# Modulation loads issued by GpSimd, and three groups of layer 0's output projection moved from whole to three-pass products

## The chip, the cores and the metric

The kernel runs on one core of a Trainium2 chip. A core has a matrix engine (TensorE, PE), a vector engine (VectorE, DVE), a scalar engine (ScalarE, ACT), GpSimd (POOL) and SyncE (SP), each with a list of instructions of its own that it works through in order. Sixteen DMA engines carry the transfers that an engine's list starts. The metric is the device time of one execution in microseconds (us), as the median of several runs.

## The reference

A decoder trunk of two layers, width 2048, 256 tokens, all in float32. Cut to what matters:

```python
c_act = silu(c)
for l in range(2):
    mod = c_act @ w_mod[l] + b_mod[l]                  # 2048 x 12288 per layer
    shift1, scale1, gate1, shift2, scale2, gate2 = split(mod, 6)
    h = rms_norm(x, norm1_gain[l]) * (1 + scale1) + shift1
    x = x + gate1 * mixer(h, w_in[l], ..., w_out[l])   # one input and one output projection
    h = rms_norm(x, norm2_gain[l]) * (1 + scale2) + shift2
    x = x + gate2 * (silu(h @ w_gate[l]) * (h @ w_up[l])) @ w_down[l]   # inner width 5632
return rms_norm(x, final_norm_gain)
```

The mixer cuts the projected columns into three sorts of heads: gated linear attention (GLA, 512 output columns), sliding-window softmax attention with sinks (1024 columns) and gated DeltaNet (512 columns). Their outputs stand side by side, 2048 wide, and go through `w_out`.

## The kernel before, in words

The 256 tokens are two blocks of 128 rows. All weights are read from HBM once, in tiles of 128 rows by up to 1024 columns (512 KB).

The order of the work is that of the Python code, as a scheduler turns it into one list for each engine: it takes the code's order as priority and fills each engine's list by its own estimate of when things are ready. Each list is then fixed, and an instruction in it waits by semaphores for data and for free buffers. A DMA stands in the list of the engine that issues it, and whatever is behind it in that list waits with it.

*Weights.* `stream()` walks jobs (a pair of 512-column segments, an index k of 128 rows), and `load()` inside it issues each weight tile on SP (L323). There are two forms of product:

- three-pass: the tile `raw` is rounded to `wh` by ScalarE (L330), VectorE forms the rest `wl` = `raw` - `wh` (L331), and PE adds three products in a fast rounded format (`wh` with both halves of the activations, `wl` with one). `raw` has 3 buffers, `wh` and `wl` 3 each.
- whole: the tile is multiplied as it is, in plain float32, each product as two PE instructions in the trace; nothing is rounded or split. The tiles then take turns in the buffers of `raw`, `wh` and `wl`, nine in all.

For the output projection the constant `WHOLE_OUT` names, by layer, the groups of four k whose products are whole: group 0 is GLA (k 0 to 3), 1 and 2 are softmax attention (k 4 to 11), 3 is DeltaNet (k 12 to 15). The projection has 16 k and two halves of 1024 columns, so 32 jobs, k 4 to 15 first. Activations of a three-pass group are split in the same way, by `split_mix`, between softmax attention and GLA.

*Modulation.* `mod_segment` computes `c_act @ w_mod` for one stretch of columns. For each 128 rows it loads a tile of `w_mod` (L220), and VectorE multiplies it by a column of `c_act` and adds it to an accumulator (L223). The accumulator is cleared by GpSimd (L212), and its first row is filled with `b_mod` by a 4 KB load (L213). When all 16 steps are done, PE sums over the partitions (L238 for gates, L248 for the others), into `fin`; VectorE turns that into columns `mod` (L250 to L256).

Layer 0's first shift and scale are "early": 512 columns wide, 256 KB loads, tiles named `g`, 128 loads in all. The other 20 segments have 1024 columns and 16 loads of 512 KB each, named `mraw` (2 buffers) and `acc` (2 buffers). They are spread over the other work: `tick()` is called as the streams go on and releases a step at a rate that depends on the stage (`RATE_A`, `RATE_OUT`, `RATE_FFN` and the like). `hold` ties one load after each second norm to the norm's end, by a tiny GpSimd copy into its buffer (L218). Before the change SP issues all of these loads, between the weights.

*GpSimd* also computes the inverse square roots of all norms (L408), the negated sinks (L891) and some clears.

Of the kernel before, what the change touches and what calls it, by code (L numbers as in the profile page):

```python
# [19 lines left out]
P = 128  # L20
# [22 lines left out]
WHOLE_IN = (True, False)  # L43
WHOLE_A = (3, 0)
RATE_LAST = 1.6
WHOLE_OUT = ((0, 1, 2, 3), ())
XN_ACT = ((False, False), (False, False))

FIN_LAG = 4
# [54 lines left out]
def trunk(ctx: ExitStack, tc, x, cT, pos, small, consts, b_mod, w_mod, w_in, w_gk, w_out,  # L104
# [22 lines left out]
    def tl(pool, shape, tag, dt=F32, bufs=None):  # L127
        return pool.tile(shape, dt, tag=tag, name=nm(tag), bufs=bufs)
# [11 lines left out]
    V, A, G, TE, SY = nc.vector, nc.scalar, nc.gpsimd, nc.tensor, nc.sync  # L140
# [41 lines left out]
    for name, turn in (("sin", 0.0), ("cos", 0.25)):  # L182
        n = tl(kp, [P, NB, 8], "turns" + name)
# [17 lines left out]
    def mod_segment(l, part, k0, nk):  # L201

        width = nk * P
        early = l == 0 and part in (SHIFT1, SCALE1)
        rows = (512 if early else 1024) // width
        st = {}

        def step(i):
            c0 = part * D + k0 * P
            if i == 0:  # L210
                st["acc"] = scr[1]() if early else tl(accp, [P, 1024], "acc")
                G.memset(st["acc"][:, :width], 0.0)  # L212
                SY.dma_start(st["acc"][0:1, :width], b_mod[l:l + 1, c0:c0 + width])  # L213
            acc = st["acc"][:, :width]
            n = min(rows, KD - i)
            raw = scr[1]() if early else tl(modp, [P, 1024], "mraw")
            if hold:
                G.tensor_copy(raw[:, 0:1], hold.pop())  # L218
            raw = raw[:, :n * width].rearrange("p (a n) -> p a n", a=n)
            SY.dma_start(raw, w_mod[l, i * P:(i + n) * P, c0:c0 + width]  # L220
                         .rearrange("(a p) n -> p a n", p=P))
            for a in range(n):
                V.scalar_tensor_tensor(acc, raw[:, a], c_act[:, i + a:i + a + 1], acc,  # L223
                                       ALU.mult, ALU.add)
            if i + n == KD:
                fins.append([FIN_LAG, lambda: finish(acc)])

        def finish(acc):
            if part in (GATE1, GATE2):
                g = tl(gatep, [P, 1024], "gate")  # L230
                for j in range(width // 512):
                    src = acc[:, j * 512:(j + 1) * 512]
                    t = tl(modp, [P, 2, 512], "mraw", F32R)
                    A.activation(t[:, 0], src, AF.Copy)
                    V.tensor_tensor(t[:, 1], src, t[:, 0].bitcast(F32), ALU.subtract)
                    ps = tl(psf, [P, 512], "fin")
                    for i in range(2):
                        TE.matmul(ps, ones_r, t[:, i], start=i == 0, stop=i == 1)  # L238
                    A.activation(g[:, j * 512:(j + 1) * 512], ps, AF.Copy)
                    gate_row[l, part, k0 // 4 + j] = g[:, j * 512:(j + 1) * 512]  # L240
                return
            t = tl(smp, [P, nk], f"mod{part}_{k0}_{nk}")
            sums = tl(smp, [P, nk], f"sums{nk}")
            for j in range(0, nk, 4):
                ps = tl(psf, [P, 512], "fin")
                n = min(4, nk - j)
                for i in range(n):
                    TE.transpose(ps[:, i * P:(i + 1) * P],  # L248
                                 acc[:, (j + i) * P:(j + i + 1) * P], ident)
                V.tensor_reduce(sums[:, j:j + n],  # L250
                                ps[:, :n * P].rearrange("p (a b) -> p a b", a=n), AX.X, ALU.add)
            if part in (SHIFT1, SHIFT2):
                V.tensor_copy(t, sums)
            else:
                o = (0 if part == SCALE1 else KD) + k0
                V.scalar_tensor_tensor(t, sums, 1.0, gains[:, l, o:o + nk],  # L256
                                       ALU.add, ALU.mult)
            for j in range(nk):
                mod_col[l, part, k0 + j] = t[:, j:j + 1]

        return [((l, part), lambda i=i: step(i)) for i in range(0, KD, rows)]


# [113 lines left out]
    def ahead(wsp_n, hm_n):  # L377
        return (None,) * wsp_n + (at_hm,) * hm_n
# [7 lines left out]
    def split(src, scale=None):  # L386

        h = tl(hmp, [P, 4, P], "hm", F32R)
        lo = tl(hmp, [P, 4, P], "hm", F32R)
        h2, lo2 = (t.rearrange("p a b -> p (a b)") for t in (h, lo))  # L390
        if scale is None:
            A.activation(h2, src, AF.Copy)
            V.tensor_tensor(lo2, src, h2.bitcast(F32), ALU.subtract)
        else:
            A.activation(h2, src, AF.Copy, scale=scale)
            V.scalar_tensor_tensor(lo2, src, scale, h2.bitcast(F32), ALU.mult, ALU.subtract)
        return h, lo
# [91 lines left out]
    def to_mix(l, key, ps, gain=None):  # L489
        if key[1] == 0 and 0 not in WHOLE_OUT[l]:  # L490
            mix[key] = split(ps, gain)
            return
        t = mix[key] if key in mix else tl(hmp, [P, 4, P], "hm")
        A.activation(t.rearrange("p a b -> p (a b)"), ps, AF.Copy,
                     scale=1.0 if gain is None else gain)
        mix[key] = t
# [23 lines left out]
    def split_mix(l, group):  # L520
        if group not in WHOLE_OUT[l]:
            for blk in range(NB):
                mix[blk, group] = split(mix[blk, group].rearrange("p a b -> p (a b)"))
# [425 lines left out]
    def layer(l):  # L949
# [158 lines left out]
        for ks in (range(4, 16), range(0, 4)):  # L1108
            final = ks[0] == 0
            if final:  # L1110
# [3 lines left out]
                           blk, j, ps, half, final)) for half in range(2)]  # L1114
            stream(groups, ks, lhs_mix, whole=[k for k in ks if k // 4 in WHOLE_OUT[l]],
                   tail=() if not final else TAIL_WHOLE if 0 in WHOLE_OUT[l] else
                   ahead(*TAIL_OUT))
# [100 lines left out]
```

## Time and profile before

| | us |
|---|---|
| median of 3 runs (2582.32 to 2587.12) | 2582.44 |
| the profiled execution | 2585.34 |
| its span | 2583.5 |
| PE busy | 2432.7 |
| VectorE busy | 1714.4 |
| ScalarE busy | 1053.5 |
| GpSimd busy | 58.2 |

The mean granted PE clock was 0.986 of full. Windows give, for a stretch of the span, each engine's busy time with its instructions in brackets (PE, its weight loads PEld, DVE, ACT, POOL), then the granted clock, the mean busy share of the 16 DMA engines and GB/s. A row of a group of instructions gives line, engine, operation, result <- operands, shapes and count; busy time and mean ns; idle time of the engine just ahead of them and what ended it. A row of waits gives total us, times and the longest. A timeline row gives start, duration, engine, line, operation, and in brackets the idle time ahead of it and what ended that. SPq is the list of DMAs on SP.

The stages by the span's time: early modulation and input projection of layer 0 to 390 us, GLA and output projection to 560, second norm to 592, FFN of layer 0 to 1360; input projection of layer 1 from 1390 to 1510, its attention, GLA and output projection to 1830, its FFN to 2560.

### The profile page before, as it was taken

What the parts mean: (1) busy time and instruction counts of PE and PEld (TensorE: products, weight loads), DVE (VectorE), ACT (ScalarE), POOL (GpSimd) and SP (SyncE); (2) the same over time, 40 slices, a digit from 0 to 9 for tenths busy, and PEclk for the clock granted to TensorE, in tenths of its full rate; (3) what the DMA queues carried; (4) which work ended last, traced back from release to release, by engine and by line L of the source; (5) the groups of instructions that cost most, each with busy time, mean ns of one, the idle gap of its engine ahead of it and who ended that gap; (6) DMA issues with size and microseconds to landing.
All of it is one profiled execution on the core that took longest, in us unless ns stands there. A gap on an engine that the chain in (4) does not pass through costs nothing.

```text
span 2583.5 us, 30803 instructions
## 1 busy us (share of the span) xinstructions
PE 2432.7 (94%) x11164; PEld 1884.1 (73%) x11164; DVE 1714.4 (66%) x2171; ACT 1053.5 (41%) x1548; POOL 58.2 (2%) x117
## 2 busy tenths in 40 slices
PE   4999998889999988999999999999999999999998
PEld 2555785447878767788877878877778878888876
DVE  6767867576675777657578785888664575544555
ACT  2203443124444333344335454564644434344443
POOL 1000000000000000000000000000000000000000
PEclk9999999989999999999999999999999999999999
DMA  9996538777778888868687861675676686666654
GB/s 341 368 322 204 180 114 282 258 231 268 261 259 260 283 268 274 292 193 286 223 277 261 281 192 50 214 232 192 212 256 193 200 286 195 188 191 188 189 184 155
DMA packets 190033, 600.79 MB, mean 233 GB/s; under 512 B 21628, under 2 KB 26268, under 8 KB 189496
## 3 DMA queue, kind: packets, MB, share of 16 engines
q1 hardware_dynamic: 189880, 598.81, 70.7%
q8 instruction: 88, 1.44, 0.2%
q14 instruction: 65, 0.53, 0.1%
HBM read 596.63 MB, written 2.10 MB: 232 GB/s over the span
## 4 chain that ended last, share of the span: by engine, by line
PE 57%; DMA 20%; DVE 10%; issue 8%; ACT 4%; POOL 1%; SPq 1%; DVEq 0%; ACTq 0%; POOLq 0%
PE acc L358 48%; DMA mraw<-in_w_mod 13%; DVE wl L331 4%; DMA raw<-in_w_down 3%; DMA raw<-in_w_in 2%; DVE acc L223 2%; ACT wh L330 1%; PE mm L403 1%; PE ga L895 1%; DMA raw<-in_w_up 1%; PE mm L678 1%; PE mm L685 1%; PE ga L916 1%; DMA raw<-in_w_gate 1%; PE fin L248 1%
## 5 line engine op out<-in xcount | busy, mean ns | idle before, releaser
L358 PE MATMUL acc<-wh,hm 128*128 128x512 f32 (+3 forms) x4872 | 1339.2, 389 | 20.9 <-DVE xs L931 4.7
L330 ACT ACTIVATE wh<-raw 128x1024 fp32r<-128x1024 f32 (+3 forms) x669 | 684.7, 1025 | 985.8 <-PE acc L358 548.9
L331 DVE TENSOR_TENSOR wl<-raw,wh 128x1024 fp32r<-128x1024 f32 (+3 forms) x669 | 785.2, 1179 | 446.6 <-ACT wh L330 444.5
L358 PEld LDWEIGHTS acc<-wh,hm 128*128 128x128 f32 x4872 | 892.0, 189 | 215.8 <-issue 25.5
L358 PE MATMUL acc<-wl,hm 128*128 128x512 f32 (+3 forms) x2484 | 792.3, 394 | 12.2 <-DVE wl L331 9.7
L223 DVE SCALAR_TENSOR_TENSOR acc<-mraw,c_act,acc 128x1024 f32<-128x1024 f32 x320 | 410.3, 1282 | 225.2 <-DMA mraw<-in_w_mod 222.9
L358 PEld LDWEIGHTS acc<-wl,hm 128*128 128x128 f32 x2484 | 458.4, 190 | 124.1 <-DVE wl L331 22.3
L358 PE MATMUL acc<-wh,ahl 128*128 128x512 f32 x560 | 158.4, 397 | 0.0
L358 PEld LDWEIGHTS acc<-wh,ahl 128*128 128x128 f32 x560 | 105.8, 189 | 24.5
L358 PE MATMUL acc<-wl,ahl 128*128 128x512 f32 x280 | 90.8, 398 | 7.2 <-DVE wl L331 7.2
L223 DVE SCALAR_TENSOR_TENSOR g<-g,c_act,g 128x512 f32<-128x512 f32 x128 | 88.7, 747 | 12.6 <-DMA g<-in_w_mod 12.4
L358 PE MATMUL acc<-wh,b 128*128 128x512 f32 (+2 forms) x184 | 74.7, 545 | 2.2 <-ACT b L447 2.1
L358 PE MATMUL acc<-wl,b 128*128 128x512 f32 (+2 forms) x176 | 67.1, 518 | 2.6 <-DVE g L969 2.6
L358 PEld LDWEIGHTS acc<-wl,ahl 128*128 128x128 f32 x280 | 52.2, 189 | 23.1 <-DVE wl L331 11.3
L358 PE MATMUL acc<-raw,b 128*128 128x512 f32 (+2 forms) x176 | 67.6, 524 | 0.0
L358 PEld LDWEIGHTS acc<-wh,b 128*128 128x128 f32 x184 | 35.2, 197 | 30.8 <-issue 23.1
L358 PEld LDWEIGHTS acc<-wl,b 128*128 128x128 f32 x176 | 32.8, 192 | 29.2 <-issue 20.3
L416 ACT ACTIVATE acc<-xs 128x512 f32<-128x512 f32 x32 | 19.0, 595 | 85.7 <-DVE xs L931 85.7
L447 ACT ACTIVATE b<-mm,mod,mod 128x128 f32<-128x128 f32 x24 | 9.2, 461 | 109.7 <-DVE mod L256 92.1
L358 PEld LDWEIGHTS acc<-raw,b 128*128 128x128 f32 x176 | 33.5, 195 | 26.7 <-issue 21.7
L929 DVE TENSOR_TENSOR acc<-acc,gate 128x512 f32<-128x512 f32 x64 | 43.0, 695 | 10.3 <-PE acc L358 10.2
L358 PE MATMUL acc<-raw,hm 128*128 128x512 f32 x88 | 41.7, 598 | 1.4 <-ACT acc L416 1.4
(314 smaller groups left out, 1645.8 us busy)
## 6 DMA issues: line engine op xcount, KB each, us to landing
mraw<-in_w_mod SPq DMA_DIRECT2D x320, 512.0 KB
raw<-in_w_down SPq DMA_DIRECT2D x176, 512.0 KB
raw<-in_w_gate SPq DMA_DIRECT2D x160, 512.0 KB
raw<-in_w_up SPq DMA_DIRECT2D x160, 512.0 KB
raw<-in_w_in SPq DMA_DIRECT2D x72, 512.0 KB
g<-in_w_mod SPq DMA_DIRECT2D x128, 256.0 KB
raw<-in_w_out SPq DMA_DIRECT2D x43, 512.0 KB
raw<-in_w_in SPq DMA_DIRECT2D x32, 264.0 KB
```

The costliest lines, as they stand in the source:

```text
L223: V.scalar_tensor_tensor(acc, raw[:, a], c_act[:, i + a:i + a + 1], acc, ALU.mult, ALU.add)
L248: TE.transpose(ps[:, i * P:(i + 1) * P], acc[:, (j + i) * P:(j + i + 1) * P], ident)
L330: A.activation(wh[:, :width], raw[:, :width], AF.Copy)
L331: V.tensor_tensor(wl[:, :width], raw[:, :width], wh[:, :width].bitcast(F32), ALU.subtract)
L358: TE.matmul(ps[blk, j][:, :segs[j][2]], xa, parts[j][part], start=i == 0 and n == 0, stop=last and n == len(terms) - 1)
L403: TE.transpose(ps[:, j * P:(j + 1) * P], src[:, j * P:(j + 1) * P], ident)
L416: A.activation(scr[0]() if junk is None else junk, xs[:, blk, j * 512:(j + 1) * 512], AF.Square, accum_out=ssq[blk][:, j:j + 1])
L678: TE.matmul(ps[:, s], LT[blk][:, s], Tm[blk][:, s], start=True, stop=True)
L685: TE.matmul(ps[:, s], U[blk][:, s], m1[:, s], start=True, stop=True)
L895: TE.matmul(ps[:, j * nk:(j + 1) * nk], qT[rows, i + j], kT[rows, g, :nk], start=True, stop=True)
L916: TE.matmul(ps[:, j * 64:(j + 1) * 64], pT[:, j * nk + kb * P:j * nk + (kb + 1) * P], kv[kb][:, P + g * 64:P + (g + 1) * 64], start=kb == ...
L929: V.tensor_tensor(ps, ps, need(gate_row, (l, part, j)), ALU.mult)
```

## The change

The 1024-column modulation loads (320 of 512 KB) and their 20 bias rows are issued by GpSimd (`G`) instead of SP (`SY`). The early ones stay on SP. And `WHOLE_OUT` of layer 0 keeps GLA alone: 24 of the 32 jobs (12 k, two halves) become three-pass, and the activations of groups 1, 2 and 3 are split, in 6 tiles of 512 columns.

```diff
-WHOLE_OUT = ((0, 1, 2, 3), ())
+WHOLE_OUT = ((0,), ())
...
                 G.memset(st["acc"][:, :width], 0.0)
-                SY.dma_start(st["acc"][0:1, :width], b_mod[l:l + 1, c0:c0 + width])
+                (SY if early else G).dma_start(st["acc"][0:1, :width], b_mod[l:l + 1, c0:c0 + width])
...
-            SY.dma_start(raw, w_mod[l, i * P:(i + n) * P, c0:c0 + width]
-                         .rearrange("(a p) n -> p a n", p=P))
+            (SY if early else G).dma_start(raw, w_mod[l, i * P:(i + n) * P, c0:c0 + width]
+                                           .rearrange("(a p) n -> p a n", p=P))
```

The scheduler makes new lists from this. SP's list goes from 1341 to 1001 rows, GpSimd's from 122 to 462. The early part of SP's list keeps its order, less the `mraw` loads.

GpSimd at the start, before: `acc` are the accumulators of the first two 1024-column segments, the first `g` and the last are those of the first two early ones, and `rms` are the inverse square roots of the first norm.

```order
L212 MEMSET g_205 128x512
L212 MEMSET acc_1231 128x1024
L212 MEMSET acc_2032 128x1024
L212 MEMSET g_211 128x512
L408 ISA
L408 TENSOR_TENSOR rms_38_179<-ss_37_176,half_100 128x1
L408 TENSOR_TENSOR rms_45_193<-ss_44_190,half_100 128x1
```

GpSimd at the same place, after:

```order
L212 MEMSET acc_1231 128x1024
L220 DMA mraw_1234<-in_w_mod 128x1024
L213 DMA acc_1231<-in_b_mod 1x16x64
L220 DMA mraw_1243<-in_w_mod 128x1024
L212 MEMSET acc_2032 128x1024
L213 DMA acc_2032<-in_b_mod 1x16x64
L220 DMA mraw_1246<-in_w_mod 128x1024
L212 MEMSET g_211 128x512
L220 DMA mraw_1255<-in_w_mod 128x1024
L220 DMA mraw_1268<-in_w_mod 128x1024
L408 ISA
L408 TENSOR_TENSOR rms_38_179<-ss_37_176,half_100 128x1
```

The clear of the second early accumulator `g_211` now stands behind the third modulation load, which needs one of two buffers back, and the square roots behind the fifth. SP's second bias row (into `g_211`) waits for that clear.

VectorE at the start, before: `ss` is the first norm's sum of squares, `g` are early accumulations.

```order
L421 TENSOR_REDUCE ss_37_176<-ssp_32_167 128x1
L422 TENSOR_SCALAR ss_37_176<-ss_37_176 128x1
L223 SCALAR_TENSOR_TENSOR g_205<-g_208,c_act_102,g_205 128x512
L223 SCALAR_TENSOR_TENSOR g_211<-g_214,c_act_102,g_211 128x512
L421 TENSOR_REDUCE ss_44_190<-ssp_39_181 128x1
```

VectorE there, after:

```order
L223 SCALAR_TENSOR_TENSOR acc_1231<-mraw_1234,c_act_102,acc_1231 128x1024
L223 SCALAR_TENSOR_TENSOR acc_1231<-mraw_1243,c_act_102,acc_1231 128x1024
L223 SCALAR_TENSOR_TENSOR acc_1231<-mraw_1246,c_act_102,acc_1231 128x1024
L421 TENSOR_REDUCE ss_37_176<-ssp_32_167 128x1
L223 SCALAR_TENSOR_TENSOR g_205<-g_208,c_act_102,g_205 128x512
L422 TENSOR_SCALAR ss_37_176<-ss_37_176 128x1
```

Three 1024-column accumulations come ahead of the first norm, and 20 have been done when block 2's `mod` (the second group of four columns of layer 0's first shift) is computed; before, there was none until all of the early ones were done. From the end of layer 0's input projection on, the counts at the same places agree within three up to the end of layer 0's FFN; layer 1's input projection then has 12 more ahead of DeltaNet.

VectorE in GLA of layer 0, before (one of its levels: `a`, `ga` and `mm` are GLA's own):

```order
L831 COPY_PREDICATED a_3188<-masks_90,ga_3229 128x512
L831 COPY_PREDICATED a_3189<-masks_90,mm_3230 128x512
L804 TENSOR_TENSOR a_3245<-a_3163,a_3241 128x64x4
L804 TENSOR_TENSOR a_3245<-a_3156,a_3241 128x64x4
L795 TENSOR_TENSOR a_3260<-a_3186 128x512
L250 TENSOR_REDUCE sums_889_3476<-fin_3477 128x4
L223 SCALAR_TENSOR_TENSOR acc_3433<-mraw_3508,c_act_102,acc_3433 128x1024
```

The same place, after:

```order
L831 COPY_PREDICATED a_3212<-masks_90,ga_3253 128x512
L831 COPY_PREDICATED a_3213<-masks_90,mm_3254 128x512
L804 TENSOR_TENSOR a_3269<-a_3187,a_3265 128x64x4
L804 TENSOR_TENSOR a_3269<-a_3180,a_3265 128x64x4
L795 TENSOR_TENSOR a_3284<-a_3210 128x512
L223 SCALAR_TENSOR_TENSOR acc_3481<-mraw_3595,c_act_102,acc_3481 128x1024
L331 TENSOR_TENSOR wl_3649<-raw_3646,wh_3648 128x1024
```

Behind the accumulation of a level there is now also the subtract of an output projection tile; nine stand inside GLA's levels, eleven behind them, the rest ahead.

## The prediction

> **What bounds the kernel now.** I read the page first: its parts on engines and on groups of instructions.
>
> ```profile
> span 2583.5 us, 30803 instructions
> PE 2432.7 (94%) x11164; PEld 1884.1 (73%) x11164; DVE 1714.4 (66%) x2171; ACT 1053.5 (41%) x1548; POOL 58.2 (2%) x117
> L331 DVE TENSOR_TENSOR wl<-raw,wh 128x1024 fp32r<-128x1024 f32 (+3 forms) x669 | 785.2, 1179 | 446.6 <-ACT wh L330 444.5
> L223 DVE SCALAR_TENSOR_TENSOR acc<-mraw,c_act,acc 128x1024 f32<-128x1024 f32 x320 | 410.3, 1282 | 225.2 <-DMA mraw<-in_w_mod 222.9
> ```
>
> TensorE (PE) is busy for 94% and idle for 151 us. A saving must come out of that idle time or out of PE's own work. VectorE (DVE) stood for 222.9 us in front of modulation loads. Next the windows by stage: busy time, then clock, DMA share and GB/s.
>
> ```profile
> 41.00:160.00 119.00, 118.22 (x364) 65.85 (x365) 87.91 (x146) 19.76 (x47) 2.73 (x16) 1.00 1.01 367
> 160.00:260.00 100.00, 97.36 (x314) 54.69 (x312) 69.32 (x162) 28.53 (x55) 4.31 (x4) 0.95 0.67 228
> ...
> 390.00:485.00 95.00, 86.34 (x431) 52.02 (x432) 69.15 (x104) 31.01 (x65) 4.33 (x4) 1.00 0.83 275
> 485.00:560.00 75.00, 65.57 (x154) 28.52 (x152) 47.71 (x52) 6.19 (x15) 1.56 (x2) 0.95 0.82 269
> 560.00:592.00 32.00, 24.17 (x92) 18.20 (x93) 20.20 (x34) 20.57 (x48) 2.78 (x4) 0.73 0.32 102
> 592.00:900.00 308.00, 298.81 (x1319) 241.37 (x1318) 211.41 (x189) 129.79 (x138) 1.91 (x2) 1.00 0.82 274
> 900.00:1110.00 210.00, 193.73 (x820) 153.75 (x818) 142.75 (x133) 73.39 (x72) 1.90 (x2) 0.98 0.82 273
> ...
> 1200.00:1360.00 160.00, 154.39 (x679) 123.49 (x678) 109.96 (x109) 65.01 (x75) 0.95 (x1) 1.00 0.78 259
> ...
> 1390.00:1510.00 120.00, 114.08 (x636) 96.98 (x635) 93.47 (x143) 57.60 (x83) 0.00 (x0) 1.00 0.87 283
> ...
> 1830.00:1930.00 100.00, 96.90 (x427) 78.07 (x426) 68.48 (x63) 45.86 (x52) 0.72 (x1) 0.99 0.79 267
> ...
> 2060.00:2140.00 80.00, 77.19 (x346) 63.04 (x345) 56.41 (x52) 33.03 (x35) 0.00 (x0) 1.00 0.81 277
> 2140.00:2560.00 420.00, 416.94 (x1841) 341.15 (x1841) 214.81 (x203) 175.95 (x188) 0.00 (x0) 1.00 0.61 189
> ```
>
> At 41 to 160 us both PE and the DMA engines are full. From 592 to 1360 (layer 0's FFN, modulation loads beside weights) PE idles 9.2 + 16.3 + 5.6 = 31 us, while at 2140 to 2560, where no modulation runs, only 3.1 of 420. Why it idles, the SyncE queue's (SPq) waits and one example show:
>
> ```profile
> SPq L220 <- DVE acc L223: 221.4, 162, 4.4
> SPq L220 <- DMA mraw<-in_w_mod: 92.2, 80, 3.6
> ...
> 900.15 5.61 SPq L323 DMA_DIRECT2D raw<-in_w_down  x2
> 905.82 0.42 SPq L220 DMA_DIRECT2D mraw<-in_w_mod  x1
> ...
> 907.99 1.28 DVE L223 SCALAR_TENSOR_TENSOR acc<-mraw,c_act,acc 128x1024 f32<-128x1024 f32 x1 [2.58 <-DMA mraw<-in_w_mod]
> ...
> 910.47 0.72 PE L358 MATMUL acc<-wl,ahl 128*128 128x512 f32 x2 [1.95 <-DVE wl L331]
> ```
>
> It is a loop. SP's weight load waits for a buffer; the modulation load behind it goes out 5.6 us later; DVE waits for that load 2.58 us; the subtract behind it is late; PE waits 1.95 us.
>
> **The change, part by part.**
>
> *Start, +26 us.* GpSimd's (POOL's) order now begins with modulation loads: 20 of 512 KB are accumulated before block 2's `mod`, where before there were none. At the start:
>
> ```profile
> 5.04 0.24 SPq L213 DMA_DIRECT2D g<-in_b_mod  x1
> 5.32 26.05 SPq L220 DMA_DIRECT2D g<-in_w_mod  x31
> ...
> 13.31 0.96 POOL L408 TENSOR_TENSOR rms<-ss,half 128x1 f32<-128x1 f32 x1 [9.19 <-DVE ss L422]
> ...
> 94.93 4.72 DVE L223 SCALAR_TENSOR_TENSOR g<-g,c_act,g 128x512 f32<-128x512 f32 x7
> ...
> 112.80 1.41 DVE L223 SCALAR_TENSOR_TENSOR g<-g,c_act,g 128x512 f32<-128x512 f32 x2
> ...
> 114.35 0.60 PE L248 MATMUL fin<-consts,g 128*128 128x128 f32 x4
> ```
>
> The last accumulation before block 3's transposes ends 0.1 us ahead of them; nothing covers a later load. 20 x 524,288 bytes at 367 GB/s are 28.6 us. I take off 2.5 for the little that DVE has in hand: +26. Low end +21 (at 94.93 seven early accumulations run without a wait: 4.7 us more in hand); high end +33 (the second bias row, issued at 5.04, now waits for a memset that stands behind the third modulation load; 5 to 7 us with SP's 31 loads behind it). DVE's 20 x 1.28 = 26 us more lie inside the longer stretch: it is idle 31 of 119. Paid back at 160 to 260: at most PE's idle 2.6; I take -2.
>
> *Output projection of layer 0, -4 us.* 24 of its 32 jobs change form. A whole job is 8 instructions, a three-pass one 12 shorter ones:
>
> ```profile
> 502.45 3.60 PE L358 MATMUL acc<-raw,hm 128*128 128x512 f32 x8
> 505.89 3.60 PE L358 MATMUL acc<-wh,hm 128*128 128x512 f32 x8
> ...
> 2299.73 1.07 PE L358 MATMUL acc<-wh,hm 128*128 128x512 f32 x4
> 2300.64 0.62 PE L358 MATMUL acc<-wl,hm 128*128 128x512 f32 x2
> 2301.09 1.07 PE L358 MATMUL acc<-wh,hm 128*128 128x512 f32 x4
> ```
>
> From start to start that is 3.44 us against 2 x 1.36 = 2.72: PE saves 24 x 0.72 = 17 us. DVE gains 24 subtracts of 1.22 us (below) and 6 of 512 columns, half that by estimate: 33 us. ScalarE (ACT) gains 24 roundings of about that length and 6 halves, some 30 us, into 58 busy of 202 us: hidden. From 390 to 592 PE was busy 176 of 202 and DVE 137; now 159 and 170. DVE becomes the longer:
>
> ```profile
> 440.00:450.00 10.00, 9.15 (x50) 4.64 (x49) 9.91 (x18) 2.85 (x5) 0.95 (x1) 1.00 0.88 304
> ...
> L331 DVE TENSOR_TENSOR wl<-raw,wh 128x1024 fp32r<-128x1024 f32 x148 | 181.1, 1225 | 196.8 <-ACT wh L330 196.8
> L223 DVE SCALAR_TENSOR_TENSOR acc<-mraw,c_act,acc 128x1024 f32<-128x1024 f32 x128 | 164.3, 1283 | 114.3 <-DMA mraw<-in_w_mod 113.3 <-DMA acc<-in_b_mod 0.2
> ```
>
> (the two groups are of 2140 to 2560 and of 592 to 1360). Filled as PE filled it (176/202), 170 us need 195: -7. But 9 subtracts, 11 us, fall into GLA's levels, where DVE has nothing free. I take -4; ends -17 (PE's whole saving) and +10 (those 11 us).
>
> *The hold at norm 2, -5 us.* The first load of a held buffer now blocks POOL, not SP:
>
> ```profile
> 574.65 14.83 SPq L220 DMA_DIRECT2D mraw<-in_w_mod  x2
> 589.57 1.60 SPq L323 DMA_DIRECT2D raw<-in_w_gate  x2
> ```
>
> For 14.8 us no gate weight could be issued. Of the 7.8 us idle at 560 to 592 and PE's later start I take -5 (layer 1's norm 2 is in the next term); ends 0, since the norm itself sets most of the stage, and -8.
>
> *FFN layers, -18 us.* SP is left with weights; a modulation load goes out as soon as its buffer is free, so the loop above opens. At the undisturbed rate (3.1/420) the 768 us would idle 5.6: at most 25 of the 31 us come back. The two modulation buffers stay, DVE stays in order, and the bytes stay, so I take -15. Layer 1's two stretches idle 5.9, of which 4.6 could go; with its hold, -3. Ends -33 and 0.
>
> *Layer 1's input projection, +3 us.* DVE's order has 12 more accumulations before DeltaNet: 6.3 MB, 17 us at 367 GB/s, into 120 us with a DMA share of 0.87 (15.6 us free). Ends -5 (PE's idle 5.9) and +12.
>
> *GpSimd itself, +3 us.* No row shows a transfer issued there. The nearest is SP's issue at 905.82, 0.42 us; POOL's own small operation takes 0.96. 340 issues by 1 us are 340 of 2583 us on an engine that is busy 58, so they are hidden unless they stand ahead of one of 14 square roots or sinks: 14 x 0.4 to 14 x 1 is 6 to 14 us, half of it beside other PE work. I take +3; ends 0 and +14. SP's 340 saved issues are worth nothing by themselves.
>
> Sum: 26 - 2 - 4 - 5 - 18 + 3 + 3 = +3. The profiled execution took 2585.3 us (its span and 1.8), 2.9 over the median of 2582.4: 2588.3 there, so 2585.4 against the median.
>
> The row that decides the FFN term is SP's 221.4 us of waiting for modulation buffers. The Trainium skill, DMA: Bandwidth & Descriptors, section Issuing engines are not separate DMA queues, says that issuing from several engines "will only save the time on the sequencer". By that rule the hold and FFN terms are nothing, +26 us in all or 2608, close to the slower rival below; the wait row speaks against it, since it is no issue time. The same page's section SWDGE vs HWDGE vs iDMA says that GpSimd builds descriptors in software; no row here shows it.
>
> **The rivals.**
> - *Slower: the loads on GpSimd give nothing back.* DVE still waits for each load because two buffers are all it has, and weights share the same 16 engines. Hold -2, FFN 0, projection 0: 26 - 2 - 2 + 3 + 3 = +28, 2610. For it: the DMA share is already 0.82 in the FFN. Against, a stretch with more bytes in which PE is full:
>
> ```profile
> 700.00:720.00 20.00, 20.00 (x90) 16.55 (x89) 14.05 (x12) 9.75 (x12) 0.00 (x0) 1.00 0.88 318
> ```
>
>   It decides if DVE's 113 us of waits for `mraw` in layer 0's FFN stay above 90.
> - *Faster: the loop was the whole loss.* Start +21, back -2, projection -17, hold -8, FFN -29, layer 1 0, GpSimd 0: -35, 2547. For it: the example at 900 to 910 us.
> - *The change doesn't do what it says at the start:* the 20 loads take only gaps, +5 in place of +26: 2564. Against: a DMA share of 1.01 leaves no gap, and DVE's order forces them.
>
> **How the numbers follow.** Cancelling 0.46 (2585, own range 2566 to 2601), slower 0.28, faster 0.20, no price at the start 0.06. A change within 0.2%, 5.2 us, is about what a measurement can't tell from none. Of the first case 0.12 lies below 2577, 0.20 within, 0.14 above: faster 0.12 + 0.20 + 0.06 = 0.38, same 0.20, slower 0.42. The range reaches from 2553 to 2614: a tenth is left out at each end.
>
> **What would show it.** Right: PE starts block 2 to 4 some 25 us later with the DMA share still at 1; by 260 us it has not caught up; the hold no longer leaves SP idle; SP's waits for `acc` L223 are gone and DVE's for `mraw` fall by half; DVE is the fuller engine from 413 to 592. Wrong: start punctual; FFN windows as before; or square roots on POOL that wait for issues.

## The result, and the profile after

| | before | after |
|---|---|---|
| median, us | 2583.57 (4 runs, 2582.32 to 2587.12) | 2706.29 (4 runs, 2695.09 to 2714.43) |
| span of the profiled execution | 2583.5 | 2712.7 |

The ratio is 1.047, with a 95% interval of [1.0429, 1.0511]: slower by 123 us, where +3 was forecast and 2553 to 2614 given as the range. The profiled execution is the slowest of the four, 8 us over their median.

Page of the changed kernel, the rows that answer to those of before:

```profile
PE 2462.5 (91%) x11260; PEld 1925.9 (71%) x11260; DVE 1745.7 (64%) x2201; ACT 1081.8 (40%) x1578; POOL 238.2 (9%) x457
...
q1 hardware_dynamic: 143760, 430.94, 47.7%
q0 software_dynamic: 46720, 167.88, 19.3%
...
L223 DVE SCALAR_TENSOR_TENSOR acc<-mraw,c_act,acc 128x1024 f32<-128x1024 f32 x320 | 410.0, 1282 | 235.3 <-DMA mraw<-in_w_mod 226.9
L220 POOL DMA_DIRECT2D mraw<-in_w_mod x320 | 170.6, 533 | 1379.4 <-DVE acc L223 868.0
...
mraw<-in_w_mod POOLq DMA_DIRECT2D x320, 512.0 KB, 4.7
```

The 168 MB of modulation went over to a queue of their own (q0). Issuing one costs GpSimd 0.53 us, and 4.7 us pass until it has landed. VectorE stands in front of these loads for as long as before: 226.9 us against 222.9. PE is idle for 250 us (span less busy) where it was 151.

Where the time went can be read from the inverse square roots on GpSimd, which stand at the seams of the stages. Timeline of GpSimd, before (DeltaNet's end, GLA's end, second norm of layer 0, first norm of layer 1, its q and k norm, its second norm, the final norm):

```profile
368.15 1.03 POOL L408 TENSOR_TENSOR grs<-gss,half 128x4 f32<-128x4 f32 x1 [10.89 <-DVE gss L508]
...
473.08 1.01 POOL L408 TENSOR_TENSOR grs<-gss,half 128x4 f32<-128x4 f32 x1 [6.59 <-DVE gss L508]
...
572.74 0.56 POOL L408 TENSOR_TENSOR rms<-ss,half 128x1 f32<-128x1 f32 x1 [11.07 <-DVE ss L422]
...
1369.98 0.55 POOL L408 TENSOR_TENSOR rms<-ss,half 128x1 f32<-128x1 f32 x1 [2.07 <-DVE mod L253]
...
1519.10 2.91 POOL L408 TENSOR_TENSOR qkrs<-qkss,half 128x16 f32<-128x16 f32 x1 [145.48 <-DVE qkss L596]
...
1822.66 0.56 POOL L408 TENSOR_TENSOR rms<-ss,half 128x1 f32<-128x1 f32 x1 [11.57 <-DVE ss L422]
...
2576.73 0.54 POOL L408 TENSOR_TENSOR rms<-ss,half 128x1 f32<-128x1 f32 x1 [10.04 <-DVE ss L422]
```

The same, after:

```profile
385.57 1.02 POOL L408 TENSOR_TENSOR grs<-gss,half 128x4 f32<-128x4 f32 x1 [11.56 <-DVE gss L508]
...
512.15 2.00 POOL L408 TENSOR_TENSOR grs<-gss,half 128x4 f32<-128x4 f32 x1 [4.04 <-DVE gss L508]
...
613.41 0.57 POOL L408 TENSOR_TENSOR rms<-ss,half 128x1 f32<-128x1 f32 x1 [2.80 <-DVE ss L422]
...
1445.78 0.57 POOL L408 TENSOR_TENSOR rms<-ss,half 128x1 f32<-128x1 f32 x1 [1.11 <-DVE mod L253]
...
1621.90 2.93 POOL L408 TENSOR_TENSOR qkrs<-qkss,half 128x16 f32<-128x16 f32 x1 [18.07 <-DVE qkss L596]
...
1933.02 0.55 POOL L408 TENSOR_TENSOR rms<-ss,half 128x1 f32<-128x1 f32 x1 [11.57 <-DVE ss L422]
...
2701.69 0.54 POOL L408 TENSOR_TENSOR rms<-ss,half 128x1 f32<-128x1 f32 x1 [9.99 <-DVE ss L422]
```

The differences from seam to seam:

| stage | before, us | after, us | more | forecast |
|---|---|---|---|---|
| start to DeltaNet's end, layer 0 | 368.2 | 385.6 | +17 | +24 |
| GLA, layer 0 | 104.9 | 126.6 | +22 | } |
| output projection and second norm | 99.7 | 101.3 | +2 | } -9 together |
| FFN, layer 0 | 797.2 | 832.4 | +35 | -15 |
| input projection, layer 1 | 149.1 | 176.1 | +27 | +3 |
| rest of layer 1's attention | 303.6 | 311.1 | +8 | 0 |
| FFN, layer 1 (with its norm) | 754.1 | 768.7 | +15 | -3 |

They add up to 125 us; the forecast's +3 for GpSimd itself stands in no single stage. The loss is spread over every stage in which modulation runs.

Waits in layer 0's FFN (us in total, times, longest), after, 640 to 1435 us:

```profile
POOL mraw L220 <- DVE acc L223: 359.5, 118, 9.7
...
DVE acc L223 <- DMA mraw<-in_w_mod: 105.3, 88, 3.9
...
PEld acc L358 <- DVE wl L331: 47.3, 35, 4.4
...
PE acc L358 <- DVE wl L331: 32.9, 25, 3.9
```

and before, 592 to 1360 us:

```profile
DVE acc L223 <- DMA mraw<-in_w_mod: 113.3, 88, 3.6
...
PEld acc L358 <- DVE wl L331: 24.4, 28, 2.4
...
PE acc L358 <- DVE wl L331: 12.8, 19, 1.9
```

SP no longer waits for modulation buffers; GpSimd does it instead. VectorE's waits for the loads hardly moved, and PE's own waits for the weights' rests rose from 12.8 to 32.9 us. How densely the loads stand, windows of two bursts for the accumulations alone (`mraw` on VectorE), before and then after:

```profile
640.00:700.00 60.00, 12.92 (x11) 1.00 0.79 261
800.00:860.00 60.00, 19.27 (x15) 1.00 0.87 301
```

```profile
640.00:700.00 60.00, 22.97 (x19) 0.95 0.81 290
740.00:800.00 60.00, 21.90 (x18) 1.00 0.87 300
```

Before, a burst held 11 to 15 accumulations in 60 us; after, 18 or 19. At 2.72 us to one weight job 60 us have 22 jobs; the weights alone are 190 GB/s (the stretch from 2140 us), and 19 loads in 60 us are 166 GB/s more: 356 together, next to the 367 that the engines gave at their fullest. That sum is an estimate and stays just under 367; what the two bursts after the change moved was 290 and 300 GB/s.

### The profile page after: what moved, and what is told of

It reads as the page before. It is cut to its first block, busy times and chain, and to the rows that moved or that the text cites. A ratio compares the mean times of both kernels' runs of the same rounds, so it can differ in the third digit from the quotient of the medians.

```text
span 2712.7 us, 31250 instructions
## 1 busy us (share of the span) xinstructions
PE 2462.5 (91%) x11260; PEld 1925.9 (71%) x11260; DVE 1745.7 (64%) x2201; ACT 1081.8 (40%) x1578; POOL 238.2 (9%) x457
## 4 chain that ended last, share of the span: by engine, by line
PE 46%; DMA 20%; DVE 9%; issue 7%; ACT 2%; POOL 1%; DVEq 0%; SPq 0%; POOLq 0%; ACTq 0%
PE acc L358 41%; DMA mraw<-in_w_mod 17%; DVE acc L223 4%; DVE wl L331 2%; DMA raw<-in_w_in 1%; PE mm L403 1%; DMA raw<-in_w_down 1%; ACT wh L330 1%; DMA raw<-in_w_gate 0%; PE ga L895 0%; PE ga L916 0%; DVE acc L929 0%; PE ga L403 0%; PE mm L678 0%; DMA raw<-in_w_out 0%
## 5 line engine op out<-in xcount | busy, mean ns | idle before, releaser
L358 PE MATMUL acc<-wh,hm 128*128 128x512 f32 (+3 forms) x5000 | 1388.4, 391 | 36.0 <-ACT acc L416 7.5
L330 ACT ACTIVATE wh<-raw 128x1024 fp32r<-128x1024 f32 (+3 forms) x693 | 710.1, 1027 | 1087.3 <-PE acc L358 641.5
L331 DVE TENSOR_TENSOR wl<-raw,wh 128x1024 fp32r<-128x1024 f32 (+3 forms) x693 | 813.9, 1180 | 502.4 <-ACT wh L330 501.7
L358 PEld LDWEIGHTS acc<-wh,hm 128*128 128x128 f32 x5000 | 930.1, 192 | 233.3 <-ACT wh L330 11.1
L358 PE MATMUL acc<-wl,hm 128*128 128x512 f32 (+2 forms) x2516 | 808.8, 395 | 60.1 <-DVE wl L331 59.6
L358 PEld LDWEIGHTS acc<-wl,hm 128*128 128x128 f32 x2516 | 469.9, 193 | 177.3 <-DVE wl L331 86.4
L223 DVE SCALAR_TENSOR_TENSOR acc<-mraw,c_act,acc 128x1024 f32<-128x1024 f32 x320 | 410.0, 1282 | 235.3 <-DMA mraw<-in_w_mod 226.9
L220 POOL DMA_DIRECT2D mraw<-in_w_mod x320 | 170.6, 533 | 1379.4 <-DVE acc L223 868.0
L358 PE MATMUL acc<-wh,b 128*128 128x512 f32 (+2 forms) x184 | 77.2, 560 | 12.8 <-DMA wh<-in_w_in 9.3
L408 POOL TENSOR_TENSOR rms<-ss,half 128x1 f32<-128x1 f32 x10 | 6.1, 606 | 544.5 <-DVE ss L422 543.3
L358 PEld LDWEIGHTS acc<-wl,b 128*128 128x128 f32 x176 | 32.9, 190 | 29.0 <-issue 21.5
```

Of the source, the lines that this page charges most:

```text
L220: (SY if early else G).dma_start(raw, w_mod[l, i * P:(i + n) * P, c0:c0 + width] .rearrange("(a p) n -> p a n", p=P))
L330: A.activation(wh[:, :width], raw[:, :width], AF.Copy)
L331: V.tensor_tensor(wl[:, :width], raw[:, :width], wh[:, :width].bitcast(F32), ALU.subtract)
L358: TE.matmul(ps[blk, j][:, :segs[j][2]], xa, parts[j][part], start=i == 0 and n == 0, stop=last and n == len(terms) - 1)
L408: G.tensor_tensor(out, v, half[:, :v.shape[-1]], ALU.pow)
```

## The experiments

Two theories went into the first runs. *Density* (*pacing* in the first expectations): in SP's list each modulation load stood at its place among the weights, and VectorE's list had 4 or 5 accumulations to seven weight tiles; with a queue of their own the scheduler puts them one to one, and the bursts ask for more than the DMA engines give. *Software queue*: transfers issued by GpSimd are slow in themselves. Ratios are against the kernel before on the same chip.

**One half of the change at a time.** `gpsimd_only` keeps `WHOLE_OUT` as before; `three_pass_only` keeps all loads on SP.

```diff
-WHOLE_OUT = ((0,), ())
+WHOLE_OUT = ((0, 1, 2, 3), ())          # gpsimd_only, against the changed kernel
```

> Only the issue by GpSimd; the output projection of layer 0 as before. Pacing theory (in SP's list each modulation load stood behind the weight loads of its place, 0.6 accumulations to one weight tile on VectorE; on GpSimd the scheduler puts them one to one, so that modulation and weights together ask for more than the DMA engines give): the start, FFN and input projection losses stay, only GLA's 21 us go: 2670 to 2695. Software queue theory (loads issued by GpSimd are slow in themselves): the same. Projection theory (the three-pass groups cost it, the queue is harmless): under 2610.

Measured: 2704.26 us, 1.0479 [1.0435, 1.0523].

> Only the three-pass groups 1 to 3 in layer 0's output projection; all loads on SP as before. Pacing and software queue theory: GLA and the projection alone move, 0 to +22 us: 2583 to 2605. Projection theory: 2660 or more. My forecast of this part was -4: 2579.

Measured: 2588.28 us, 1.002 [0.9995, 1.0046], no difference that can be told. The queue is all of the loss that can be told; by its interval the projection costs at most 12 us. GLA's 22 us belong to the queue too: in `gpsimd_only` GLA took 132 us (385.4 to 517.5) for 104.9, which I had expected to vanish there.

**The start.** `gate1_on_sp` lets SP load the two segments that had been pulled to the front.

```diff
-            (SY if early else G).dma_start(raw, ...
+            (SY if early or (l == 0 and part == GATE1) else G).dma_start(raw, ...
```

> As GpSimd alone, but layer 0's first gate (the two segments that were pulled to the start) is loaded by SP. Pacing theory: the start is as before (block 2's transposes at 82 us, not 116), which is worth the +17 that was left of it at 385 us; the FFN and layer 1's input projection lose as in the changed kernel, since their lists still stand one to one: 2655 to 2680, 17 under GpSimd alone. Software queue theory: 288 of 320 loads are still slow, within 10 us of GpSimd alone.

Measured: 2670.77 us, 1.0341 [1.0301, 1.0381]: 33 us under `gpsimd_only`. DeltaNet's end came at 366.1 us, as before (385.4 in `gpsimd_only`), and GLA took 8 us less. So the pulled loads cost some 33 us in all, and some 90 are left with no load pulled.

**Spacing the loads on GpSimd.** `gpsimd_paced` ties each load to the latest rounded weight tile.

```diff
             if hold:
                 G.tensor_copy(raw[:, 0:1], hold.pop())
+            elif not early and token:
+                G.tensor_copy(raw[:, 0:1], token[0])
...
                 A.activation(wh[:, :width], raw[:, :width], AF.Copy)
+                token[:] = [tl(smp, [P, 1], "token", bufs=4)]
+                A.activation(token[0], wh[:, 0:1].bitcast(F32), AF.Copy)
```

> As the run with the first gate on SP, with each load on GpSimd tied to its place among the weights: ScalarE copies one column of the latest rounded weight tile to a small token, and GpSimd copies that into the buffer before it issues the load. VectorE's list then has about 0.4 accumulations to a weight tile in layer 0's FFN, evenly spread. Pacing theory: the loss of the FFN and of layer 1's input projection goes, 2570 to 2600, with no 20 us window of more than 5 accumulations. Software queue theory: the loads are as slow as before and the token adds to it, 2655 or more.

Measured: 2837.41 us, 1.0989 [1.095, 1.1028]. Both theories missed by far. Waits of that run:

```profile
POOL mraw L220 <- ACT token L334: 1246.9, 175, 73.1
...
DVE acc L225 <- DMA mraw<-in_w_mod: 499.6, 197, 7.4
```

The spacing worked (2 to 5 accumulations in 20 us in the FFN), but GpSimd stood 1246.9 us for tokens, and VectorE, in order, 2.5 us for each of 197 loads. That the token held the loads back for too long is the likely cause, not a shown one: the run also adds small copies to ScalarE's and GpSimd's lists, and 99 accumulations fall into layer 0's FFN for 128. So this run does not test density.

**Another queue, and density on SP.** `act_queue` issues the loads on ScalarE; `sp_dense` leaves them on SP and makes the list dense.

```diff
-            (SY if early or (l == 0 and part == GATE1) else G).dma_start(raw, ...
+            (SY if early or (l == 0 and part == GATE1) else A).dma_start(raw, ...   # act_queue
...
-RATE_FFN = (0.4, 0.25)
+RATE_FFN = (1.0, 0.25)                                                             # sp_dense
```

> As the run with the first gate on SP, but the other 288 modulation loads and their bias rows are issued by ScalarE, whose DMAs go through a hardware queue like SP's. VectorE's list is nearly the same as there (one accumulation to one weight tile in the bursts). Density theory (the list's bursts ask for more than the DMA engines give, whoever issues): 2650 to 2690, within 20 of that run's 2671. Software queue theory (GpSimd's way of issuing is slow): 2580 to 2610.

Measured: 2650.07 us, 1.0261 [1.024, 1.0283].

> All loads on SP as before, but RATE_FFN of layer 0 is 1.0 for 0.4, so that VectorE's list has one accumulation to one weight tile in layer 0's FFN, in one long burst; the same loads fall into that FFN within a few. Density theory: layer 0's FFN takes the 20 us longer that it took with GpSimd: 2595 to 2610. Software queue theory: no difference from before, 2575 to 2590.

Measured: 2630.75 us, 1.019 [1.0165, 1.0215]. With the loads on ScalarE's queue 70 us of the 91 are still there: issuing from GpSimd costs some 20 us more than issuing from ScalarE. And a dense list costs 51 us even on SP's own queue, more than I expected. The two profiled executions differ by 41 us, 40 of them in layer 0's FFN (837.4 us from seam to seam, for 797.2). But the loads there did not stay the same within a few: 141 accumulations fall into it for 128, 17 us more of VectorE's work, in one long burst. So the 51 us are the price of density and of these 13 loads together. Its accumulations from 600 to 800 us, and those of before:

```profile
600.00:800.00 200.00, 74.73 (x61) 0.98 0.89 306
```

```profile
600.00:800.00 200.00, 41.24 (x34) 1.00 0.80 265
```

**Halved loads.** Here each 1024-column load brings only its first 512 columns, used for both halves, so half of these columns' modulation is left out; VectorE's work stays. On SP too the scheduler then puts the list one to one: lists and bytes are nearly alike, and only the queue differs.

```diff
-            SY.dma_start(raw, w_mod[l, i * P:(i + n) * P, c0:c0 + width]...
+            raw = raw[:, :512]
+            SY.dma_start(raw, w_mod[l, i * P:(i + 1) * P, c0:c0 + 512])    # half_sp; G or A in the others
+            srcs = [raw.rearrange("p (a n) -> p a n", a=1).to_broadcast([P, 2, 512])]
```

> As the run with the first gate on SP, but each 1024-column modulation load brings only its first 512 columns (256 KB for 512), and VectorE uses them for both halves: half of these columns' modulation is left out, VectorE's work stays. Density theory: without the excess bytes the loss goes; within 10 us of the same halving on SP. Software queue theory: the same 308 issues stay; 40 us or more above the same halving on SP. If only waiting for the single load matters: in between.

Measured: 2608.57 us, 1.0098 [1.0073, 1.0123].

> The same halving with all loads on SP. VectorE's list has now one accumulation to one weight tile here too. Both theories: 2540 to 2580, since before lost some 40 us beside the loads. It is the measure for the halved loads on GpSimd: density theory within 10 us of it, software queue theory 40 or more under it.

Measured: 2542.34 us, 0.9845 [0.9823, 0.9867].

> The halved loads again, issued by ScalarE (hardware queue of its own) where half_gpsimd used GpSimd; list and bytes as there. half_gpsimd was 66 us over half_sp at equal lists and bytes. If that is the software queue itself: 2540 to 2565, near half_sp. If it is that the loads have a queue of their own beside the weights', whichever engine: 2595 to 2615.

Measured: 2599.97 us, 1.0068 [1.0045, 1.0091]. So at nearly equal lists and half the bytes it costs 58 (ScalarE) to 66 us (GpSimd) to take the loads off the weights' queue, and the density theory alone falls. That the separate queue as such is the common cause is likely, but not shown: ScalarE has a price of its own, since its roundings of weights stand behind a load that waits for a buffer. ScalarE's waits of this kind, on SP and then on ScalarE (14.0 us on GpSimd):

```profile
ACT wh L338 <- DVE acc L231: 8.4, 7, 3.1
```

```profile
ACT wh L338 <- DVE acc L231: 126.2, 54, 5.5
```

VectorE's waits for the loads, on SP and then on GpSimd (146.1 us on ScalarE):

```profile
DVE acc L231 <- DMA mraw<-in_w_mod: 100.6, 104, 4.0
```

```profile
DVE acc L231 <- DMA mraw<-in_w_mod: 159.6, 137, 5.9
```

Slower transfers are not the reason: in layer 0's FFN the last DMA packet of a halved load ended 3.6 us after the load's issue on SP, 3.4 on ScalarE and 3.1 on GpSimd (medians).

**Depth.** If the loads come late, earlier issue should help. Four buffers of 512 columns take the space of two of 1024.

```diff
-    modp = ctx.enter_context(tc.tile_pool(name="modp", bufs=2))
+    modp = ctx.enter_context(tc.tile_pool(name="modp", bufs=4))
...
-            raw = scr[1]() if early else tl(modp, [P, 1024], "mraw")
+            raw = scr[1]() if early else tl(modp, [P, 512], "mraw")
```

> half_gpsimd with four buffers of 512 columns in the same space for two of 1024, so that a load can be issued four accumulations ahead. If its 66 us are the turn-round of two buffers (accumulate, issue 0.5 us, 3.4 us to landing, while VectorE stands in order before the next accumulation): 2545 to 2575, VectorE's waits for these loads under 60 us (160 there). If GpSimd's queue disturbs the weights' loads or the engines as such: 2595 or more.

Measured: 2540.29 us, 0.9826 [0.9805, 0.9847].

> The same four buffers with all loads on SP, as the measure for the former: 2530 to 2545, at most 10 us under half_sp, whose waits for these loads are 101 us in all.

Measured: 2508.57 us, 0.9703 [0.9689, 0.9718]. GpSimd's version gains 68 us, SP's 34, three times what I expected there. Waits on GpSimd with four:

```profile
DVE acc L231 <- DMA mraw<-in_w_mod: 32.9, 21, 5.9
```

159.6 us have become 32.9. GpSimd is 32 us over SP with four buffers, where it was 66 with two: at half the bytes, then, the turn-round of two buffers (accumulate, issue, land) is about half of the difference. At full bytes a third one fits if softmax attention gives up one of its nine buffers.

```diff
-    modp = ctx.enter_context(tc.tile_pool(name="modp", bufs=2))
+    modp = ctx.enter_context(tc.tile_pool(name="modp", bufs=3))
...
-        pb = bs.enter_context(tc.tile_pool(name=f"swa_{l}", bufs=9, ...
+        pb = bs.enter_context(tc.tile_pool(name=f"swa_{l}", bufs=8, ...
```

> The same three buffers with the loads on GpSimd (the first gate on SP). Turn-round theory: of the 91 us over before more than half go, as 68 did with four halved ones: 2600 to 2630, and still 30 to 50 above the same on SP, since on two queues the needed load shares the engines with weights that are not due yet. If the bytes in the bursts alone set it: 2660 or more.

Measured: 2658.41 us, 1.0287 [1.0261, 1.0313], against 1.0341 [1.0301, 1.0381] with two buffers: 12 us by the medians, but the intervals overlap. VectorE's waits went from 247.5 to 204.6 us.

> The kernel before with three full modulation buffers of 512 KB for two (room from one buffer less in softmax attention), all loads on SP. Turn-round theory (a load can be issued only when one of two buffers comes back, and VectorE, in order, stands for it): with halved loads, twice the buffers were worth 34 us on SP; one more full buffer about half: 2555 to 2575. If the loss on SP is only the head of its queue waiting for weights: 2575 to 2590.

Measured: 2554.44 us, 0.9877 [0.9855, 0.9899]. On SP the third buffer pays as forecast; VectorE's waits for the loads are 154.4 us, 222.9 before. On GpSimd it brings little: there the turn-round theory missed, and what holds the loads at full bytes is not shown.

> The changed kernel, three-pass groups and all, with the three buffers. Turn-round theory: the pull to the start stays or grows (35 loads stand before the first weights' needs for 20: 35 us or more), GLA, FFN and input projection gain as on GpSimd above: 2630 to 2670. If the bytes alone set it: 2690 or more.

Measured: 2694.34 us, 1.0423 [1.0394, 1.0452], beside the changed kernel's 1.047 [1.0429, 1.0511]: no clear difference. DeltaNet's end is at 423.2 us there (more loads are pulled to the start), and GLA is back to 105.8, with 17 accumulations in it for 31.

> Loads on SP, three buffers, three-pass groups 1 to 3: the one half of the change that cost nothing, with the buffer. Turn-round theory: as sp_3buf within 10 us, 2550 to 2580; the faster of the two is the version to keep.

Measured: 2572.1 us, 0.9937 [0.9918, 0.9957], 18 us slower than `sp_3buf`: with the third buffer the three-pass groups do cost something.

> Only softmax attention's buffers, eight for nine, two modulation buffers as before: the measure for sp_3buf. Within 5 us of before if the third modulation buffer is what sp_3buf gained by; 20 us or more under before if it was the shifted lists.

Measured: 2587.31 us, 1.0028 [1.0013, 1.0044]: the control gains nothing, so the 32 us of `sp_3buf` are the third buffer's, with the lists that come of it.

> The kernel before with four full modulation buffers (softmax attention's down from nine to six), all loads on SP. sp_3buf was 32 us under before. Turn-round theory: the fourth buffer is worth less than the third, 2540 to 2560. If softmax attention then stands for its buffers: 2560 to 2590.

Measured: 2555.71 us, 0.9901 [0.9884, 0.9918], no better than three. The version to keep is the kernel before with three modulation buffers, 1.2% faster than before and 5.6% faster than the change.

## Why the prediction was wrong, point by point

*Step that failed: "FFN layers, -18 us".* It said that a modulation load would go out as soon as its buffer is free, "so the loop above opens". The first half came: SP's 221 us of waiting are gone, and in layer 0's FFN a load goes out 0.3 us after its buffer comes free, for 1.5 before (medians). The second did not: VectorE's waits for `mraw` there are 105.3 us for 113.3, and the two FFNs lost 35 and 15 us (17 and 16 in `gpsimd_only`, whose list for the FFN is nearly the same).

The loop was misread from its own example. With two buffers in turn, the accumulation at 907.99 takes the load issued at 899.33. The load issued at 905.82 is for the accumulation after it (before):

```profile
899.33 0.42 SPq L220 DMA_DIRECT2D mraw<-in_w_mod  x1
...
912.00 1.28 DVE L223 SCALAR_TENSOR_TENSOR acc<-mraw,c_act,acc 128x1024 f32<-128x1024 f32 x1 [0.41 <-DMA mraw<-in_w_mod]
```

So VectorE began 8.7 us after the issue of the load that it stood for. The 5.6 us of SP's weight loads came behind that issue. Its buffer had come free at 897.78, so an open queue could have sent it 1.5 us earlier, not 5.6; the rest of its way was transfer.

Two more things were missing. I took from the lists how many accumulations fall into each stage, and these counts agree; I did not look at their spacing inside a stage, which the same lists show, and which went from 4 or 5 accumulations to seven weight tiles to about 7. `sp_dense`, as dense but in one long burst and with 13 more loads in it, costs 51 us on SP's own queue. And I took SP's queue for a hindrance alone: the halved loads show 58 to 66 us between it and another, with the lists nearly alike. What in the other queue costs this stays open. How the loss at full bytes divides between the two stays open: the run that was to space the loads on GpSimd slowed them in another way, and a third buffer gained little there.

The Trainium skill, DMA: Bandwidth & Descriptors, section Issuing engines are not separate DMA queues, has transfers of all engines interleave on the same 16 DMA engines. By that a load on GpSimd has no engines of its own, and shares them with the weights. No row here shows the interleaving, and the halved loads landed no later after their issue on GpSimd than on SP (3.1 and 3.6 us), so it does not explain their price. The section's other half, that several issuers only save issue time, gave 2608 in the prediction, and the measurement is about 100 us beyond it.

*Start, +26: mis-sized, at its high end.* PE's transposes of blocks 2, 3 and 4 (before at 82.27, 114.35 and 149.13):

```profile
115.68 0.60 PE L248 MATMUL fin<-consts,g 128*128 128x128 f32 x4
...
148.71 0.60 PE L248 MATMUL fin<-consts,g 128*128 128x128 f32 x4
...
183.25 0.60 PE L248 MATMUL fin<-consts,g 128*128 128x128 f32 x4
```

They are 33, 34 and 34 us late. The price of the blocked queue, which I kept for the high end, agrees with that, as SP's list shows:

```profile
14.16 0.23 SPq L213 DMA_DIRECT2D g<-in_b_mod  x1
14.43 28.81 SPq L220 DMA_DIRECT2D g<-in_w_mod  x31
```

The second bias row went out at 14.16 for 5.04, 9 us late, with the 31 loads behind it. "Paid back at most 2.6" was wrong the other way: 17 us had been paid back by DeltaNet's end. From block 4's transposes to there PE was idle for 2.2 us and busy for 200, where it had been idle for 7.2 and busy for 212, at a mean granted clock of 0.99 for 0.96. That the 20 accumulations no longer stand behind the early part is the likely reason (VectorE was busy for 125 us there, for 153). Net +17 where +24 was summed.

*Output projection, -4:* `three_pass_only` measured +5 by its ratio, with an interval that holds zero; the term stands within its range, -17 to +10. With the third buffer it was +18 (`three_pass_sp_3buf` against `sp_3buf`), past that end. GLA's +22 us came from the queue, not from the subtracts that the high end held.

*Hold, -5: no gain to be seen.* SP did issue gate weights through the norm, but the stage from GLA's end to the norm, which holds the output projection too, took 101.3 us for 99.7 (95.8 in `gpsimd_only`). That the norm itself sets this stage, the end that I had named, fits, but no run isolates it.

*Layer 1's input projection, +3: it was +27.* Twelve more loads were read from the list, 17 us of DMA time, of which I hid all but a few in the free share. ScalarE's waits for weights in this stage, after (1446 to 1622 us) and before (1370 to 1519):

```profile
ACT wh L330 <- DMA raw<-in_w_in: 69.1, 32, 6.5
```

```profile
ACT wh L330 <- DMA raw<-in_w_in: 40.8, 28, 5.2
```

With halved loads the two stages differ by 4 us between GpSimd and SP (153.5 and 149.7 from seam to seam), so the size of the loads matters here. Their number explains little: between these seams stand 31 accumulations before and 43 after, but `act_queue` has 34 and still took 169.0 us, and `sp_dense` has 19 and took 148.1, where before took 149.1. So the term failed as the FFN's did: it priced the loads by their count, and most of the loss came with the queue.

*GpSimd itself, +3:* the issue took 0.53 us, inside the bounds of 0.4 to 1. The 288 loads cost some 20 us more from GpSimd than from ScalarE (2671 and 2650); what either costs by itself is not shown.

*The rivals.* The slower one came, with its deciding mark (waits above 90: 105.3), but it stopped at "nothing given back". That the loads could do harm on their new queue was no case of mine, so 2614 was too low an end.

## What to carry to other kernels

Moving loads to a queue of their own is not free, even where the old queue often waits: with halved loads and nearly equal lists it cost 58 to 66 us here. Read the spacing of the new lists, not the counts by stage. Where an in-order engine stands for a load, first try one more buffer on the old queue: here that gained 32 us. A long wait of a queue for a buffer is not a price; look at who is late because of it, and follow the late instruction back to its own load, not to the nearest one.

## What the runs showed of the hardware that was not expected

PE loses more than the wait itself. After a 3.95 us wait in layer 0's FFN its matmuls ran at about half speed for some 5 us (timeline of PE, after):

```profile
693.96 1.07 PE L358 MATMUL acc<-wh,hm 128*128 128x512 f32 x4
698.98 1.22 PE L358 MATMUL acc<-wl,hm 128*128 128x512 f32 x2 [3.95 <-DVE wl L331]
700.00 1.91 PE L358 MATMUL acc<-wh,hm 128*128 128x512 f32 x4
701.71 1.05 PE L358 MATMUL acc<-wl,hm 128*128 128x512 f32 x2
702.56 1.89 PE L358 MATMUL acc<-wh,hm 128*128 128x512 f32 x4
704.26 0.65 PE L358 MATMUL acc<-wl,hm 128*128 128x512 f32 x2
704.75 1.08 PE L358 MATMUL acc<-wh,hm 128*128 128x512 f32 x4
```

Four matmuls took 1.91 us for 1.07, and the granted clock of 700 to 720 us was 0.89. Over that FFN the mean granted clock was 0.97 for 0.99, and PE was busy 774 us for 760 with the same number of instructions (3322 and 3323): 14 of the 35 us are the clock's, and the other 21 are idle time. My sum priced idle time only.
